# Gate and up products of an expert in one run, and its waiting steps in one place

## The chip, the cores and the metric

The kernel runs on one core of one Trainium2 chip. The time is device microseconds, the median of several runs. TensorE (PE) multiplies, VectorE (DVE) and ScalarE (ACT) work element by element, GpSimd (POOL) does small jobs, and SyncE (SP) issues the transfers (DMAs) from HBM. PSUM holds the products: eight banks of 128 partitions by 512 fp32.

## The reference

Two residual layers on 272 tokens of 1024 features: each has a token mixer, and then a channel mixer, which is a dense SwiGLU in layer 0 and eight experts in layer 1, of which each token uses two. The change is in the experts alone. For every expert e:

```python
def swiglu(x, wg, wu, wd):
    return (jax.nn.silu(x @ wg) * (x @ wu)) @ wd

for e in range(N_EXPERTS):                       # 8
    out = out + comb[:, e:e + 1] * swiglu(xt, wg[e], wu[e], wd[e])
```

`wg` and `wu` are 1024 x 3584, `wd` is 3584 x 1024, all fp32; `comb` holds the routing weights and is zero where a token doesn't use the expert. After the experts comes a last norm, of 256 tokens.

## The kernel before

**The stream of weights.** All weights come in the order of their use as units of 1 MiB (128 x 2048 fp32), one DMA each on SyncE's queue (class `Stream`). In the experts' stage sixteen buffers are used in turn (`raw`, `xh`, `xl`, `lt`, `mg`), and two units more land once in `nh` and `nl`. A buffer is free when `st.release(u)` is called behind the last matmul that reads it; the call also issues the next DMA into it, and SyncE waits there until TensorE has got so far. An expert has 42 units, 336 in all.

**An expert.** Each expert takes only the tokens that are routed to it, gathered into slots. Experts are ordered by their number of tokens. Those of kind "B" (0, 2, 3, 5, 6) have 96 slots, those of kind "S" (1, 4, 7) have 64. An expert goes through its hidden features in seven steps j of 512. The products of a step are gate (1024 features by 512, 2 units), up (the same) and down (512 by 1024, 2 units), in the order gate_up(0), gate_up(1), down(0), gate_up(2), down(1), ..., gate_up(6), down(5), down(6).

**Two ways through a product.** Weights are the moving operand, slots the stationary one. A unit has 4 blocks of 128 x 512, a product 8. Slots 1 to 64 are worked off by `halves`: per block two matmuls with 64 stationary columns, side by side in TensorE's columns. Slots 65 to 96 go through `quarters`: four with 32 columns. Each fp32 matmul leaves two records in the trace, so a product has 32 records of halves (L1214) and 64 of quarters (L1219). For a large expert `products` goes through the 8 blocks in one way and then in the other, and the next product begins in the way in which the last one ended (`turns`). For a small one there are halves only. A buffer is released in the second way over its blocks.

**Steps between.** `products` calls `between()` once, in a large expert between the two ways, in a small one after 4 blocks of 8. There stands other TensorE work: `hidden` transposes the last step's activations (L1316, 2 or 3 matmuls), which the next down product needs, and `spare_time(n)` takes n entries off the list `pending`. These are `by_slot` (L1109, and L1115 for expert 0: one-hot rows by slot, turned by TensorE), `scatter` (L1263: results of the expert before, added to the tokens), the ranking of the experts, and empty entries, which keep a scatter from being reached before its results are split:

```python
def between():
    if m and last:
        hidden(*last)
    spare_time(2 - m)
...
if not final and d == 0:
    pending.extend([lambda: None] * 2)
```

So a gate product has up to two entries in its middle, an up product the transposes and one, a down product one. Between the last two down products at the end of a group of experts stand the matmuls that gather the next group's tokens (L1089). The order on every engine is the program's; nothing is reordered.

Of the kernel before, what the change touches and what calls it, by code (L numbers as in the profile page):

```python
# [18 lines left out]
KD = D // P  # L19
# [15 lines left out]
SMALL = 64  # L35
MORE = CAP - SMALL
# [171 lines left out]
def _build(ctx, tc, nc, A, out, dbg):  # L208
    V, S, G, PE = nc.vector, nc.scalar, nc.gpsimd, nc.tensor
    w = A["w"]  # L210
    NRAW, NHL, NRAWB, NRAWC = 6, 3, 4, 2

    def units_of(pool, n):
        return [lambda: pool.tile([P, UNIT], F32, name="raw")] * n
# [26 lines left out]
    def bank(tag):  # L241
        return psum.tile([P, 512], F32, name=tag, bufs=BANKS[tag])
# [8 lines left out]
    st = Stream(nc, w, units_of(rawp, NRAW), hlp, NHL, 0, dbg.get("units", UNITS))  # L251
# [739 lines left out]
    def one(shape, dt, nm):  # L991
        return mo.tile(shape, dt, name=nm, bufs=1)

    acc = [[one([P, 512], F32, f"hacc{t}{d}") for d in range(2)] for t in range(2)]
# [46 lines left out]
    def spare_half(name):  # L1041

        return hlp.tile([P, HALF], F32R, name=name, bufs=NHL + (name == "whi"))

    pending = []
# [165 lines left out]
    def halves(a, x, w, start, stop):  # L1211

        for g in range(2):
            PE.matmul(a[g * SMALL:(g + 1) * SMALL, :256], lhsT=x, rhs=w[:, g * 256:(g + 1) * 256], start=start, stop=stop)  # L1214

    def quarters(a, x, w, start, stop):

        for r in range(4):
            PE.matmul(a[r * MORE:(r + 1) * MORE, 256:384], lhsT=x, rhs=w[:, r * P:(r + 1) * P], start=start, stop=stop,  # L1219
                      tile_position=(0, r * MORE))  # L1220

    turns = [0]

    def products(st, small, a, x, y, start, stop, between):

        blocks, u = st.pair()
        ways = [0] if small else [turns[0], 1 - turns[0]]
        for n, way in enumerate(ways):  # L1230
            for k, w in enumerate(blocks):
                if n == len(ways) - 1 and k == (4 if small else 0):
                    between()
                at, begin, end = a(k), start(k) and n == 0, stop(k) and n == len(ways) - 1
                if way:
                    quarters(at, y(k), w, begin, end)
                else:
                    halves(at, x(k), w, begin, end)
                if n == len(ways) - 1 and k % 4 == 3:
                    st.release(u + k // 4)  # L1240
        turns[0] = ways[-1]


# [2 lines left out]
    def split_y(run, q, d, a):  # L1246

        parts = []
        for y, n, c0, cw in ((YA, SMALL, 0, 256), (YB, MORE, 256, P))[:1 if run.small(q) else 2]:
            for i in range(P // n):  # L1250
                c = slice(i * cw, (i + 1) * cw)
                parts.append((y[:n, d, c], y[n:2 * n, d, c], a[i * n:(i + 1) * n, c0:c0 + cw]))
        for hi, lo, src in parts:
            S.activation(hi, src, AF.Copy)
        for hi, lo, src in parts:
            V.tensor_tensor(lo, src, hi.bitcast(F32), op=OP.subtract)
# [45 lines left out]
    pending = []  # L1302

    def experts(st, run, first):

        hid, dn_, oht = {}, {}, {}

        def hidden(q, j):

            h = hid.get((q, j), ())  # L1310
            if len(h) == 1:
                w = run.width(q)
                h.append(spare_half("whi")[:, :384].bitcast(F32))
                p = bank("acc")
                for b in range(w // P):
                    PE.transpose(p[:, b * P:(b + 1) * P], h[0][:, b * P:(b + 1) * P], ident)  # L1316
                V.tensor_copy(h[1][:, :w], p[:, :w])  # L1317

        def spare_time(n):
            for _ in range(n):  # L1320
                if pending:
                    pending.pop(0)()

        def gate_up(q, j, last):
            gu = []
            n, w = run.slots(q), run.width(q)
            x = run.x[q]

            for m in range(2):
                a = bank(("acc", "s")[m])  # L1330

                def between():
                    if m and last:
                        hidden(*last)
                    spare_time(2 - m)

                products(st, run.small(q), lambda k: a, lambda k: x[:, k, :SMALL], lambda k: x[:, k, SMALL:],
                         lambda k: k == 0, lambda k: k == KD - 1, between)
                gu.append(a)
            s = me.tile([P, 384], F32, name="es")  # L1340
            if first and q == 0:
                for i, c in enumerate((slice(0, 256), slice(256, 384))):
                    r = rs[:, i:i + 1]
                    S.activation(s[:, c], gu[0][:, c], AF.Silu, scale=r)
                    V.scalar_tensor_tensor(s[:, c], gu[1][:, c], r, s[:, c], op0=OP.mult, op1=OP.mult)
            else:
                S.activation(s[:, :w], gu[0][:, :w], AF.Silu)  # L1347
                V.tensor_tensor(s[:, :w], gu[1][:, :w], s[:, :w], op=OP.mult)  # L1348
            hid[q, j] = [s]

        def down(q, j, between):
            h = hid[q, j][1]

            def x(k):
                o = k % 2 * P + k % 4 // 2 * SMALL
                return h[:, o:o + SMALL]

            products(st, run.small(q), lambda k: dn_[q][k // 4], x, lambda k: h[:, 256 + k % 4 * MORE:256 + (k % 4 + 1) * MORE],
                     lambda k: j == 0 and k % 4 == 0, lambda k: j == FJ - 1 and k % 4 == 3, between)

        def results(q, d, final):

            split_y(run, q, d, dn_[q][d])
            if not final and d == 0:
                pending.extend([lambda: None] * 2)
            pending.extend([lambda t=t: scatter(run, q, oht[q], t, d, "acc" if final or t else "o") for t in range(2)])
            if final:
                pending.append(lambda: square_sums(d))

        for q in range(NEXP):  # L1370
            final = q == NEXP - 1
            i = run.group[q]
            turnover = q == run.groups[i][-1] and not final
            last = None
            oht[q] = mo.tile([P, 4 * P], F32R, name="oht")
            if q == 0:
                pending.append(lambda: run.by_slot(0, oht[0], first))
                if first:
                    ranking = rank_steps()
                    pending.extend([lambda: next(ranking)] * 8)  # L1380
            for j in range(FJ):
                gate_up(q, j, last)
                last = (q, j)
                if first and q == 0 and j == FJ - 4:
                    load_order()
                    for n in range(4):
                        pending.append(lambda n=n: again_by_tokens(n // 2, n % 2))
                if turnover and j == FJ - 2:
                    run.onehot(i + 1)
                if j == 0:  # L1390
                    continue
                if j == 1:
                    dn_[q] = [bank("t"), bank("t")]
                    if q:
                        pending.append(lambda q=q: run.by_slot(q, oht[q]))

                def between():
                    if j == FJ - 1:
                        hidden(q, j)
                    spare_time(1)  # L1400

                down(q, j - 1, between)
                if final and j == FJ - 2:
                    pending.extend([lambda d=d: g_final(d) for d in range(2)])
            if turnover:
                for c2 in range(4):
                    run.gather(i + 1, c2, ("s", "acc")[c2 % 2])
            if final:
                spare_time(len(pending))
                S.activation(mx_, ssq, AF.Sqrt)  # L1410
                XG["fin"] = st.spare().rearrange("p (t d f) -> p t d f", t=2, d=2)

            def between():
                if final and run.small(q):
                    results(q, 0, final)

            down(q, FJ - 1, between)
            for d in range(1 if final and run.small(q) else 0, 2):
                results(q, d, final)
        while pending:  # L1420
            pending.pop(0)()
        result()
# [147 lines left out]
```

## Time and profile before

| | |
|---|---|
| time, median of 3 runs | 1620.93 us (1620.39 to 1622.29) |
| the profiled execution | 1621.91 us, span 1620.2 us |
| TensorE busy | 1592.5 us (98%) |
| VectorE, ScalarE, GpSimd busy | 614.3, 464.5, 132.4 us |
| read from HBM | 468.93 MB |
| expert 0 begins | 752.70 us after the span's start |

Times in the rows below count from the span's start. A row of the timeline gives start, duration, engine, line, operation, what is written and read, the shape, and how many records are merged. Matmuls' ends are modelled, so starts are compared, not ends. The granted clock is a share of 2.4 GHz. The DMA share is the mean busy share of 16 DMA engines.

### The profile page before, as it was taken

The numbers are of one execution on the slowest core, as the hardware profiler recorded it, in microseconds if no ns is written. First come the engines' busy times: TensorE is split into PE (matmuls) and PEld (weight loads), VectorE is DVE, ScalarE is ACT, GpSimd is POOL, SyncE is SP. The second block draws the span as 40 slices with busy tenths as digits, with TensorE's granted clock in tenths as the row PEclk, the third lists the DMA queues.
The fourth block names the chain that finished last, engine by engine and source line by source line (L and its number), as shares of the span: only waits on it lengthen the run. The fifth ranks groups of instructions, "written<-read, shape, count | busy, mean of one in ns | idle before, by whom it ended". The sixth has DMA issues, their size and how long they took to land.

```text
span 1620.2 us, 41035 instructions
## 1 busy us (share of the span) xinstructions
PE 1592.5 (98%) x18251; PEld 1321.8 (82%) x18251; DVE 614.3 (38%) x1124; ACT 464.5 (29%) x811; POOL 132.4 (8%) x203
## 2 busy tenths in 40 slices
PE   8999999999999999999999999999999999999995
PEld 8999999999999999998777667777766677777663
DVE  5667676655556676764112111021020210210202
ACT  5545655544444446653011000010010100100101
POOL 3201152000012002430000000000000000000000
PEclk9999999999999999999999999999999999999998
DMA  7333454444453334766989999999999999999993
GB/s 304 120 141 131 151 186 161 179 176 166 179 189 138 131 130 158 272 256 240 371 329 359 419 418 417 417 418 417 405 400 419 418 418 417 418 417 407 405 419 153
DMA packets 66288, 472.78 MB, mean 292 GB/s; under 512 B 7344, under 2 KB 7472, under 8 KB 9520
## 3 DMA queue, kind: packets, MB, share of 16 engines
q1 hardware_dynamic: 65952, 469.86, 73.6%
q8 instruction: 147, 2.41, 0.6%
q14 instruction: 45, 0.37, 0.1%
q10 hardware_dynamic: 144, 0.15, 0.0%
HBM read 468.93 MB, written 1.05 MB: 290 GB/s over the span
## 4 chain that ended last, share of the span: by engine, by line
PE 95%; DVE 2%; ACT 1%; DMA 1%; POOL 0%; issue 0%; SPq 0%; ACTq 0%; DVEq 0%; POOLq 0%
PE s L1214 12%; PE t L1214 12%; PE acc L1214 12%; PE acc L280 8%; PE acc L282 8%; PE acc L281 8%; PE acc L1219 4%; PE s L1219 4%; PE t L1219 4%; PE s L282 2%; PE s L280 2%; PE s L281 2%; PE t L281 2%; PE t L280 2%; PE t L282 2%; PE acc L1316 2%
## 5 line engine op out<-in xcount | busy, mean ns | idle before, releaser
L167 DVE TENSOR_TENSOR wlo<-raw,whi 128x1024 fp32r<-128x1024 f32 x218 | 272.4, 1250 | 35.9 <-PE acc L282 13.5
L154 ACT ACTIVATE whi<-raw 128x1024 fp32r<-128x1024 f32 x218 | 229.4, 1055 | 155.7 <-issue 51.4
L280 PE MATMUL acc<-xh,whi 128*128 128x272 f32 (+1 forms) x864 | 252.9, 293 | 0.0
L282 PE MATMUL acc<-xh,wlo 128*128 128x272 f32 (+1 forms) x864 | 248.1, 287 | 0.8 <-DVE wlo L167 0.8
L281 PE MATMUL acc<-xl,whi 128*128 128x272 f32 (+1 forms) x864 | 247.6, 287 | 0.0
L1317 DVE COPY whi<-acc 128x384 f32<-128x384 f32 (+1 forms) x56 | 28.5, 508 | 500.5 <-PE acc L1316 500.5
L1347 ACT ACTIVATE es<-acc 128x384 f32<-128x384 f32 (+1 forms) x49 | 21.8, 444 | 554.8 <-PE acc L1316 538.4
L280 PEld LDWEIGHTS acc<-xh,whi 128*128 128x128 f32 x864 | 162.9, 189 | 1.6 <-issue 0.3
L282 PEld LDWEIGHTS acc<-xh,wlo 128*128 128x128 f32 x864 | 162.9, 189 | 1.0 <-DVE wlo L167 1.0
L281 PEld LDWEIGHTS acc<-xl,whi 128*128 128x128 f32 x864 | 163.2, 189 | 0.1
L1214 PE MATMUL s<-raw,xg 128*64 128x256 f32 x1344 | 156.8, 382 | 0.0
L1214 PE MATMUL t<-raw,whi 128*64 128x256 f32 x1328 | 153.1, 381 | 0.0
L1214 PE MATMUL acc<-raw,xg 128*64 128x256 f32 x1328 | 152.5, 380 | 0.0
L1214 PEld LDWEIGHTS s<-raw,xg 128*64 128x64 f32 x1344 | 93.8, 137 | 50.2 <-issue 6.1
L1214 PEld LDWEIGHTS acc<-raw,xg 128*64 128x64 f32 x1328 | 94.1, 137 | 49.2 <-issue 3.2
L1214 PEld LDWEIGHTS t<-raw,whi 128*64 128x64 f32 x1328 | 93.6, 137 | 48.5 <-issue 3.5
L280 PE MATMUL t<-xh,whi 128*128 128x272 f32 (+1 forms) x208 | 60.0, 288 | 0.0
L282 PE MATMUL t<-xh,wlo 128*128 128x272 f32 (+1 forms) x208 | 59.8, 288 | 0.0
L281 PE MATMUL t<-xl,whi 128*128 128x272 f32 (+1 forms) x208 | 59.8, 287 | 0.0
L1348 DVE TENSOR_TENSOR es<-s,es 128x384 f32<-128x384 f32 (+1 forms) x49 | 24.5, 501 | 92.3 <-PE s L1214 71.2
L1219 PE MATMUL acc<-raw,xg 128*32 128x128 f32 x1760 | 56.1, 279 | 0.0
L280 PE MATMUL s<-xh,whi 128*128 128x272 f32 (+1 forms) x176 | 52.0, 295 | 2.5 <-ACT whi L154 2.5
(453 smaller groups left out, 2650.7 us busy)
## 6 DMA issues: line engine op xcount, KB each, us to landing
raw<-w SPq DMA_DIRECT2D x356, 1024.0 KB, 12.4
xh<-w SPq DMA_DIRECT2D x21, 1024.0 KB, 17.5
xl<-w SPq DMA_DIRECT2D x21, 1024.0 KB, 17.0
lt<-w SPq DMA_DIRECT2D x21, 1024.0 KB, 17.8
mg<-w SPq DMA_DIRECT2D x21, 1024.0 KB, 18.3
raw<-w SPq DMA_DIRECT2D x6, 512.0 KB, 7.9
hT<-hT SPq DMA_DIRECT2D x4, 272.0 KB, 6.9
lw<-lruw SPq DMA_DIRECT2D x2, 512.0 KB, 8.9
```

What stands on the lines that cost most here:

```text
L154: self.nc.scalar.activation(hi, src, AF.Copy)
L167: self.nc.vector.tensor_tensor(lo, src, hi.bitcast(F32), op=OP.subtract)
L280: PE.matmul(ps, lhsT=wh, rhs=xh, start=start, stop=False)
L281: PE.matmul(ps, lhsT=wh, rhs=xl, start=False, stop=False)
L282: PE.matmul(ps, lhsT=wl, rhs=xh, start=False, stop=stop)
L1214: PE.matmul(a[g * SMALL:(g + 1) * SMALL, :256], lhsT=x, rhs=w[:, g * 256:(g + 1) * 256], start=start, stop=stop)
L1219: PE.matmul(a[r * MORE:(r + 1) * MORE, 256:384], lhsT=x, rhs=w[:, r * P:(r + 1) * P], start=start, stop=stop, tile_position=(0, r * MORE))
L1316: PE.transpose(p[:, b * P:(b + 1) * P], h[0][:, b * P:(b + 1) * P], ident)
L1317: V.tensor_copy(h[1][:, :w], p[:, :w])
L1347: S.activation(s[:, :w], gu[0][:, :w], AF.Silu)
L1348: V.tensor_tensor(s[:, :w], gu[1][:, :w], s[:, :w], op=OP.mult)
```

## The change

`products` takes a number n of pairs of units. The gate and up products of a step become one call with n = 2: sixteen blocks in one way, then sixteen in the other (for a small expert sixteen blocks of halves). Both PSUM banks are taken at the start. `between()` is called once for both, ahead of the second way or after 8 blocks of 16, and does the transposes and up to two entries. Buffers are released as before, in the last way over their blocks. A down product stays as it was. One empty entry less is put ahead of the scatters.

```diff
-    def products(st, small, a, x, y, start, stop, between):
+    def products(st, small, n, a, x, y, start, stop, between):
-        blocks, u = st.pair()
+        pairs = [st.pair() for _ in range(n)]
+        blocks = [w for b, _ in pairs for w in b]
         ways = [0] if small else [turns[0], 1 - turns[0]]
-        for n, way in enumerate(ways):
+        for i, way in enumerate(ways):
             for k, w in enumerate(blocks):
-                if n == len(ways) - 1 and k == (4 if small else 0):
+                if i == len(ways) - 1 and k == (4 * n if small else 0):
                     between()
-                at, begin, end = a(k), start(k) and n == 0, stop(k) and n == len(ways) - 1
+                at, begin, end = a(k), start(k) and i == 0, stop(k) and i == len(ways) - 1
                 if way:
                     quarters(at, y(k), w, begin, end)
                 else:
                     halves(at, x(k), w, begin, end)
-                if n == len(ways) - 1 and k % 4 == 3:
-                    st.release(u + k // 4)
+                if i == len(ways) - 1 and k % 4 == 3:
+                    st.release(pairs[k // 8][1] + k % 8 // 4)
         turns[0] = ways[-1]
...
         def gate_up(q, j, last):
-            gu = []
             n, w = run.slots(q), run.width(q)
             x = run.x[q]
-
-            for m in range(2):
-                a = bank(("acc", "s")[m])
-
-                def between():
-                    if m and last:
-                        hidden(*last)
-                    spare_time(2 - m)
-
-                products(st, run.small(q), lambda k: a, lambda k: x[:, k, :SMALL], lambda k: x[:, k, SMALL:],
-                         lambda k: k == 0, lambda k: k == KD - 1, between)
-                gu.append(a)
+            gu = [bank("acc"), bank("s")]
+
+            def between():
+                if last:
+                    hidden(*last)
+                spare_time(2)
+
+            products(st, run.small(q), 2, lambda k: gu[k // KD], lambda k: x[:, k % KD, :SMALL], lambda k: x[:, k % KD, SMALL:],
+                     lambda k: k % KD == 0, lambda k: k % KD == KD - 1, between)
...
-            products(st, run.small(q), lambda k: dn_[q][k // 4], x, lambda k: h[:, 256 + k % 4 * MORE:256 + (k % 4 + 1) * MORE],
+            products(st, run.small(q), 1, lambda k: dn_[q][k // 4], x, lambda k: h[:, 256 + k % 4 * MORE:256 + (k % 4 + 1) * MORE],
...
             if not final and d == 0:
-                pending.extend([lambda: None] * 2)
+                pending.append(lambda: None)
```

## Rows read from the trace of the kernel before

**Rows 1.** The page: span and number of instructions.
```profile
span 1620.2 us, 41035 instructions
```

**Rows 2.** Experts 0, 2: busy PE, PEld, DVE, ACT, POOL; clock, DMA share, GB/s.
```profile
752.00:879.00 127.00, 124.51 (x2076) 93.19 (x2079) 23.13 (x72) 12.27 (x29) 0.00 (x0) 0.97 0.87 334
...
958.00:1080.00 122.00, 122.00 (x2083) 90.51 (x2083) 15.06 (x32) 6.88 (x17) 0.00 (x0) 1.00 1.01 418
```

**Rows 3.** Issues of weights from 878.7 to 1575.2 us: time to landing.
```profile
DMA to landing us min/median/max: 5.2/19.8/21.2
```

**Rows 4.** Waits of SyncE's queue, 765 to 1600 us: total, times, longest.
```profile
SPq L126 <- DMA raw<-w: 227.0, 119, 2.9
```

**Rows 5.** The one issue at 878.8 us.
```profile
L126 SPq DMA_DIRECT2D raw<-w x1: 333/333/333, 878.8 to 878.8; - x1
...
DMA to landing us min/median/max: 5.2/5.2/5.2
```

**Rows 6.** The last issue of the stream.
```profile
L126 SPq DMA_DIRECT2D raw<-w x1: 333/333/333, 1574.8 to 1574.8; - x1
...
DMA to landing us min/median/max: 20.9/20.9/20.9
```

**Rows 7.** Timeline of TensorE in the last expert.
```profile
1546.21 3.62 PE L1214 MATMUL t<-raw,whi 128*64 128x256 f32 x32
1549.66 3.62 PE L1214 MATMUL acc<-raw,xg 128*64 128x256 f32 x32
...
1554.94 0.44 PE L1316 MATMUL acc<-ident,es 128*128 128x128 f32 x2
1555.31 1.95 PE L1214 MATMUL s<-xh,xg 128*64 128x256 f32 x16
...
1565.82 0.44 PE L1316 MATMUL acc<-ident,es 128*128 128x128 f32 x2
...
1594.06 5.40 PE L1214 MATMUL t<-raw,whi 128*64 128x256 f32 x48
```

**Rows 8.** Timeline of TensorE in expert 2: a run of quarters.
```profile
974.11 1.08 PE L1219 MATMUL acc<-raw,xg 128*32 128x128 f32 x32
...
975.01 1.06 PE L1219 MATMUL acc<-xh,xg 128*32 128x128 f32 x32
...
976.76 1.06 PE L1219 MATMUL s<-lt,xg 128*32 128x128 f32 x32
...
977.75 0.55 PE L1316 MATMUL acc<-ident,es 128*128 128x128 f32 x3
```

**Rows 9.** Timeline of TensorE: transposes with a scatter behind them.
```profile
1532.19 0.44 PE L1316 MATMUL acc<-ident,es 128*128 128x128 f32 x2
1532.39 0.71 PE L1263 MATMUL acc<-wlo,oht 128*128 128x512 f32 x2
1533.03 1.95 PE L1214 MATMUL s<-raw,xg 128*64 128x256 f32 x16
```

**Rows 10.** Timeline of TensorE in expert 0's first product; in brackets idle time before.
```profile
752.70 3.67 PE L1214 MATMUL acc<-raw,xg 128*64 128x256 f32 x32
758.18 0.99 PE L1109 MATMUL o<-ident,whi 128*128 128x128 f32 x4 [1.81 <-DVE whi L1105]
759.86 1.87 PE L1115 MATMUL o<-ssq,whi 128*128 128x1 f32 x8 [0.69 <-ACT oht L1110]
761.65 3.64 PE L1219 MATMUL acc<-raw,xg 128*32 128x128 f32 x64
...
767.13 1.08 PE L1214 MATMUL s<-raw,xg 128*64 128x256 f32 x8
```

**Rows 11.** A stretch of 2 us in it: the clock is the third number from the end.
```profile
760.00:762.00 2.00, 2.00 (x16) 1.97 (x20) 0.16 (x1) 0.00 (x0) 0.00 (x0) 0.50 1.04 442
```

**Rows 12.** The one issue at 1197.1 us, at the end of expert 3.
```profile
L126 SPq DMA_DIRECT2D raw<-w x1: 333/333/333, 1197.1 to 1197.1; - x1
...
DMA to landing us min/median/max: 8.4/8.4/8.4
```

## The prediction, made before the change was run

> **What bounds the kernel now.** I read the table of stretches first, then the DMA issues one at a time, and then TensorE's timeline. All of the change lies in the experts' stage, which runs from 752.7 us almost to the end of the span [rows 1]. The reader is to see two things there. TensorE has no free time: in expert 2 it is busy for the whole stretch, 122.00 of 122.00 us [rows 2]. And the DMA engines have none either from expert 1 on: their share in that same stretch is 1.01 at 418 GB/s [rows 2], which is 2.51 us for one 1 MiB unit of weights. In the first expert alone they have room (0.87, 334 GB/s).
>
> So the question is which of the two sets the end. The issues answer it. Of the units issued between 878.8 and 1574.8 us the median takes 19.8 us to land [rows 3], nearly eight units' worth of queue, and SyncE waits 227 us for earlier transfers [rows 4]. One unit with an empty queue ahead of it takes 5.2 us: the one issued at 878.8, at the end of expert 0 [rows 5]. From that issue on the queue is never empty, so DMA time runs from there to the last landing, 1574.8 + 20.9 = 1595.7 us [rows 6], whatever TensorE does. Before it, issues wait for TensorE to free a buffer. At the far end TensorE's last run of halves, 48 records over three units, starts at 1594.06 [rows 7]; its third unit is read from about 1594.06 + 2 x 1.75 = 1597.6. That is 1.9 us after it landed.
>
> Hence two paths lead to the end. TensorE's: the sum of its work. The DMA's: the moment at which expert 0 has freed its last buffers, plus a fixed time for the units still to come, plus the tail. They are 1.9 us apart now, with TensorE the later. A TensorE gain after expert 0 is worth at most 1.9 us; a gain within expert 0 moves both.
>
> **The change, part by part.**
>
> *Fewer runs of one tiling.* A run of halves costs 3.45 us per 32 records (1546.21 to 1549.66) [rows 7]. The run from 1555.31 to the transposes at 1565.82 holds 96 records and takes 10.51 where 3 x 3.45 = 10.36 would do: 0.15 for entering and leaving. Quarters cost 1.75 us per 64 in mid-run (975.01 to 976.76) [rows 8], and the run of 128 from 974.11 to 977.75 takes 3.64 where 3.50 would do: 0.14. By the code an expert with 96 slots changes its way 21 times now and 14 times afterwards. Counting the runs in the order in which they are issued, with the steps between them, I get 88 of halves and 53 of quarters before, 64 and 37 after. That is 40 runs less, of which 36 in the five large experts: 24 x 0.15 + 16 x 0.14 = 5.8 us. In expert 0 alone it is 5 and 3, 1.2 us.
>
> The Trainium skill says that changing the tiling mode drains TensorE (TensorEngine Tiling (Array Packing), Tiling Modes, Key Properties), and puts a drain at about 128 cycles (TensorE: Matmul & The Clock Gate, Phases on the wall clock), which I estimate at 0.05 us at full clock. By that figure the 40 runs would be worth 2.1 us, and the result would come about 1 us less low; the rows show three times as much per run, and I go by them.
>
> *Steps that stand together.* Transposes followed by halves take 0.37 us (1554.94 to 1555.31) [rows 7], and followed by a scatter 0.20 (1532.19 to 1532.39) [rows 9]. Each group of steps merged with another saves 0.17. The same counting gives 82 groups before and 74 after: 1.4 us, none of it in expert 0.
>
> *The first by_slot step.* It stands in the middle of expert 0's first gate product now. Halves begin at 752.70 and would be through at 756.2, then TensorE stands still for 1.81 us, until VectorE has written the one-hot rows (758.18) [rows 10]. The granted clock then falls to its lower level, 1.2 GHz (0.50 at 760 to 762) [rows 11]. The step takes 3.47 us (758.18 to 761.65) [rows 10], and the 128 quarters after it 5.48 (761.65 to 767.13) where 3.63 is the rule: 1.85 lost. Afterwards sixteen blocks of halves come first (7.06 us, to 759.8), so VectorE is done 1.4 us before the step is reached. The wait goes (1.81), the quarters run at full clock (1.85), and the step itself shrinks. Its 0.69 us wait for ScalarE [rows 10] stays, and its records halve at most: from 3.47 to between 2.1 and 3.5. I take 2.4, so 1.1 gained. Together 4.8 us, all in expert 0.
>
> *What is added.* No instruction is. The second PSUM bank is taken 3.45 to 7 us earlier; its former reader is a product pair back, so this costs nothing. One empty entry less stands ahead of the scatters, so in a small expert the first comes behind 8 blocks of halves and not 12 (3.6 us after the previous expert's last product, not 5.3). I charge nothing, since the split that it waits for takes the same time from that product's first four blocks; without that cover the wait is 1.7 us at most, three times. Gate units are freed later in the large experts: with quarters first, the first one after 3.5 + 0.5 + 1.73 = 5.7 us of its group, not 3.5. That is 2.2 us later on SyncE's queue, behind which the next issues stand. Queued transfers cover it: where the queue is shortest, at 1197 us, a unit still takes 8.4 us to land [rows 12], against 5.2 unqueued.
>
> **The sum.** TensorE's path: 5.8 + 1.4 + 4.8 = 12.0 us less. Expert 0 has 1.2 + 4.8 = 6.0 of it. Its last product now ends with halves and not quarters, which frees its first unit 0.8 us sooner (a unit of halves takes 1.73, one of quarters 0.87), so the DMA's path begins 6.8 us sooner (the DMA engines have 0.13 x 127 = 16 us of room in that stretch to move the same units [rows 2]). With the DMA's path at -6.8 and TensorE's at -12.0, the DMA's is the later one at the end. TensorE has to wait for the last unit, and 1.8 of the 1.9 us between landing and use go as well: 6.8 + 1.8 = 8.6 us. The profiled execution took 1621.91 us, so 1613.3; it stood 1.0 us over the median of the runs (1620.93), and against that I predict **1612.3 us**. The other 3.4 us of TensorE's gain turn into waits for weights, at the beginnings of experts 2 and 5, and in the last expert.
>
> **The rivals.**
>
> *The clock stays low or falls elsewhere.* The step's 0.69 us wait stays in expert 0 and may bring the same drop a little later; for it speaks that a still stretch of 1.81 us went before the drop [rows 10, 11], against it that the stretch is now a third as long, behind 7 us of matmuls. The two losses at low clock, 1.85 and 1.1, come back: 1612.3 + 2.95 = about 1615.3. The Trainium skill has a kernel whose clock falls at each DMA wait between bursts of matmuls (TensorE: Matmul & The Clock Gate, HAM oscillation); the waits that I expect at the end would be of that kind, and no run here shows one yet. In the last expert units arrive every 2.5 us and take 1.73 to use, so TensorE would stand still for 0.8 of every 2.5 us, and a fall there would be partly covered by that waiting. Chance 0.17.
>
> *The DMA's path doesn't start sooner,* because something else than TensorE paces the issues in expert 0. For it speaks only that the share is already 0.87. Then the 1.9 us alone are to be had: 1619.1. Chance 0.12.
>
> *TensorE's whole gain counts,* if transfers run a little faster than in this profile: 1608.9. Chance 0.08.
>
> *The ring runs dry: slower.* Later freeing eats the queue in the second of two large experts in a row. It decides where a landing time falls under 5.2 + 2.2 = 7.4 us; 8.4 is the shortest seen. If the engines stood idle 2.2 us in each of the 14 groups of experts 3 and 6, that is 31 us, less the 8.6: about 1643. Against it: TensorE gains on the DMA up to there, which frees buffers sooner. Chance 0.08.
>
> **How the numbers follow.** The forecast has 0.55. The unknowns in it (the step 1.4 either way, waits up to 3 x 1.7 where they aren't covered, the run-to-run spread of 1.9) make its own range 1610 to 1615. Reaching down to the third rival and up over the first gives 1608.5 to 1617.5, leaving out 0.20. A change of 0.2%, 3.2 us, is about what a measurement of this kernel can tell from none: faster 0.80, same 0.12 (the second rival), slower 0.08 (the fourth).
>
> **What would show it.** The first by_slot step right behind 64 halves, without an idle stretch, and no low clock near 760 us. Experts' runs of up to 96 halves and 192 quarters. The last issue of expert 0 near 872 us with the queue still short, the last landing near 1589, and TensorE waits for weights in the last expert where there were none. It is wrong if the last landing stays near 1595, if landings take under 7 us in experts 3 or 6, or if the clock row shows a low stretch inside the stage.

## The result, and the profile after

The changed kernel is slower: 1639.06 us in the median of 4 runs (1637.80 to 1642.62) against 1621.28 for the kernel before on the same chip, a ratio of 1.0115 with a 95% interval of 1.0103 to 1.0127. I had predicted 1612.3, in a range that ended at 1617.5. The profiled execution took 1639.19 us, 17.3 more than the one of before.

The page's span, and its row for the queue that fetches instructions:

```profile
span 1637.4 us, 41015 instructions
...
q8 instruction: 147, 2.41, 0.6%
```

TensorE executes as many matmuls as before (18251 in both profiles). The stretches of experts 0 and 2, answering [rows 2], and of the 2 us where the clock had been low, answering [rows 11] (busy PE, PEld, DVE, ACT, POOL; then clock, DMA share, GB/s):

```profile
753.00:876.00 123.00, 120.33 (x2081) 91.13 (x2081) 22.87 (x72) 12.59 (x30) 0.00 (x0) 1.00 0.87 344
957.00:1079.00 122.00, 117.15 (x2027) 87.99 (x2027) 14.22 (x30) 6.23 (x14) 0.00 (x0) 1.00 1.01 418
...
760.00:762.00 2.00, 1.31 (x12) 0.69 (x9) 0.00 (x0) 0.60 (x1) 0.00 (x0) 1.00 0.81 332
```

The low clock near 760 us is gone (1.00 where it was 0.50). But in expert 2 TensorE, which had been busy for all of 122.00 us, now stands idle for 4.85 of them. What it waits for from 752 us to the end (who waits <- for whom: total us, times, longest):

```profile
PE s L1219 <- issue: 11.6, 11, 1.7
PE o L1109 <- DVE whi L1105: 5.8, 7, 0.9
PE acc L1317 <- issue: 2.1, 2, 1.4
PE acc L1264 <- DVE wlo L1257: 1.2, 2, 1.0
PE acc L1214 <- issue: 0.7, 2, 0.5
PE o L1115 <- ACT oht L1110: 0.7, 1, 0.7
...
```

Three of these rows, 14.4 us in 15 places, end in "issue": the instruction came late without any wait that the profile shows. The kernel before has none of them there. Its one large wait, 1.81 us for VectorE [rows 10], is gone; in its place are 5.8 us in 7 waits for the same line of VectorE.

TensorE in expert 0's first product pair, answering [rows 10]:

```profile
753.36 3.67 PE L1214 MATMUL acc<-raw,xg 128*64 128x256 f32 x32
756.86 3.62 PE L1214 MATMUL s<-raw,xg 128*64 128x256 f32 x32
760.42 0.66 PE L1109 MATMUL o<-ident,whi 128*128 128x128 f32 x4
761.76 1.05 PE L1115 MATMUL o<-ssq,whi 128*128 128x1 f32 x8 [0.69 <-ACT oht L1110]
762.74 1.95 PE L1219 MATMUL acc<-raw,xg 128*32 128x128 f32 x64
```

The step stands behind 64 halves and takes 2.32 us (760.42 to 762.74; 3.47 before), without a wait ahead of it. In expert 2 a run of 256 quarters (964.03 to 973.06) shows one of the new waits, among its last 32 records; the run of 128 in [rows 8] passes without one:

```profile
968.42 1.06 PE L1219 MATMUL acc<-xh,xg 128*32 128x128 f32 x32
969.29 1.06 PE L1219 MATMUL s<-xl,xg 128*32 128x128 f32 x32
970.16 0.60 PE L1219 MATMUL s<-lt,xg 128*32 128x128 f32 x10
972.27 0.86 PE L1219 MATMUL s<-lt,xg 128*32 128x128 f32 x22 [1.51 <-issue]
```

And the merged steps a little later, where by_slot follows transposes:

```profile
988.46 1.93 PE L1219 MATMUL s<-raw,xg 128*32 128x128 f32 x64
990.32 0.55 PE L1317 MATMUL acc<-ident,es 128*128 128x128 f32 x3
991.78 0.81 PE L1109 MATMUL o<-ident,whi 128*128 128x128 f32 x4 [0.91 <-DVE whi L1105]
992.52 3.67 PE L1214 MATMUL acc<-raw,xg 128*64 128x256 f32 x32
```

The issue at the end of expert 0 and the last issue of all, answering [rows 5, 6]:

```profile
L126 SPq DMA_DIRECT2D raw<-w x1: 333/333/333, 875.1 to 875.1; - x1
...
DMA to landing us min/median/max: 4.9/4.9/4.9
...
L126 SPq DMA_DIRECT2D raw<-w x1: 333/333/333, 1589.6 to 1589.6; - x1
...
DMA to landing us min/median/max: 19.8/19.8/19.8
```

The last unit lands at 1609.4 us. TensorE's last run of halves starts at 1611.20, so its third unit is read from about 1614.7 (two units of halves at 1.75 us later): 5.3 us of slack, where there were 1.9.

**Where the time went.** I took the starts of TensorE's records from the first expert matmul (752.70 before, 753.36 after) to the first scatter behind the last run of halves (1599.66, 1616.80), run by run, and compared each run's length with its usual one (3.45 us per 32 halves, 1.75 per 64 quarters, 0.15 or 0.14 for entering). The stage grew from 846.96 to 863.44 us:

| term | predicted, us | found, us |
|---|---|---|
| 24 runs of halves and 16 of quarters fewer | -5.8 | -5.9 |
| first by_slot: wait, clock, step | -4.8 | -4.8 |
| steps that stand together | -1.4 | +7.1 |
| runs longer than usual, nearly all at an "issue" wait | 0 | +20.1 |
| sum on TensorE's path | -12.0 | +16.5 (stage: +16.5) |

The 20.1 us are more than the view's 14.4, since it counts only what lies behind the modelled end of the matmul ahead. All 15 waits lie in quarter runs or directly behind them: in all 5 runs of 256 records, in or behind 10 of 25 runs of 192, and in none of 128.

### The profile page after: what moved, and what is told of

Read it like the earlier page. It is cut to its first block, busy times and chain, and to the rows that moved or that the text cites. A ratio compares the mean times of both kernels' runs of the same rounds, so it can differ in the third digit from the quotient of the medians.

```text
span 1637.4 us, 41015 instructions
## 1 busy us (share of the span) xinstructions
PE 1591.2 (97%) x18251; PEld 1324.1 (81%) x18251; DVE 613.4 (37%) x1124; ACT 464.1 (28%) x811; POOL 132.2 (8%) x203
## 3 DMA queue, kind: packets, MB, share of 16 engines
q8 instruction: 147, 2.41, 0.6%
## 4 chain that ended last, share of the span: by engine, by line
PE 94%; POOL 1%; issue 1%; DVE 1%; ACT 1%; DMA 1%; SPq 0%; ACTq 0%; DVEq 0%; POOLq 0%
PE acc L1214 12%; PE s L1214 12%; PE t L1214 12%; PE acc L280 8%; PE acc L282 8%; PE acc L281 8%; PE t L1219 4%; PE s L1219 4%; PE acc L1219 4%; PE s L280 2%; PE s L282 2%; PE s L281 2%; PE t L280 2%; PE t L281 2%; PE t L282 2%; PE acc L1317 2%
## 5 line engine op out<-in xcount | busy, mean ns | idle before, releaser
L1219 PE MATMUL s<-raw,xg 128*32 128x128 f32 x1760 | 57.1, 273 | 8.4 <-issue 8.4
L1219 PEld LDWEIGHTS s<-raw,xg 128*32 128x32 f32 x1760 | 49.9, 110 | 10.6 <-issue 10.6
## 6 DMA issues: line engine op xcount, KB each, us to landing
xh<-w SPq DMA_DIRECT2D x21, 1024.0 KB, 14.4
```

## The experiments

**What the two theories are.** Each of the waits has a packet of the instruction queue just ahead of or in it. The DMA queues' packets, MB and share, from 969.8 to 972.3 us around the wait above, and from 964 to 969.8 ahead of it:

```profile
q1 hardware_dynamic: 138, 1.01, 98.1%
q8 instruction: 1, 0.02, 2.7%
...
q1 hardware_dynamic: 343, 2.47, 102.7%
```

In the second stretch there is no packet of instructions. Theory A: TensorE's instructions come by DMA, some 16 KB at a time (147 packets, 2.41 MB), between the weights' packets; a long run of quarters uses them faster than they come. A run of 64 quarters is 128 instructions (each matmul has its weight load) in 1.75 us, so one in 13.7 ns, against one in 54 ns in halves (64 in 3.45 us). The rivals: sixteen blocks hold their buffers longer and starve the DMA queue; steps that stand together cost the time; long quarter runs are slow in themselves.

**e1_light: the changed kernel with little weight traffic.** Units of experts 1 to 7 are transferred with a quarter of their columns, and the matmuls read that quarter four times, so the output isn't the reference's.

```
+        elif self.next_dma >= DENSE_UNITS + EXP_UNITS:
+            self.nc.sync.dma_start(t[:, :512], self.src(self.next_dma)[:, :512])
...
+        if self.cur >= 2 * (DENSE_UNITS + EXP_UNITS):
+            o = 0
```

> The changed kernel, but each unit of weights of experts 1 to 7 is transferred with a quarter of its columns, and the matmuls read that quarter four times (so the output isn't the reference's; TensorE's instructions are the same in number, shape and order). Theory A (TensorE runs out of instructions in long runs of quarters, because their refill waits among the weights' transfers): TensorE's waits that the profile ends with "issue", 14.4 us in 15 places in the changed kernel, fall under 3 us, and the time to about 1622 us. Theory B (the refill has its own pace, whatever the other transfers do): about 14 us stay, 1639 us.

Measured: 1620.83 us in one run, where the kernel before took 1620.33 on that chip. The same expert 2 (clock, DMA share and GB/s last), and two rows of the waits:

```profile
957.00:1079.00 122.00, 121.09 (x2085) 91.12 (x2083) 15.24 (x34) 8.87 (x23) 0.00 (x0) 1.00 0.29 93
```

```profile
PE o L1114 <- DVE whi L1110: 5.8, 7, 0.9
...
PE acc L1322 <- issue: 1.0, 1, 1.0
```

The waits at issue fall from 14.4 us to 1.0 with the same instructions in the same runs. The waits for VectorE stay. So the former hang on the traffic; the latter don't.

**e2_short: sixteen blocks, but quarter runs of 128 at most.** The call for two products stays, and each call takes halves first.

```
-        ways = [0] if small else [turns[0], 1 - turns[0]]
+        ways = [0] if small else [0, 1]
```

> The changed kernel, but every product begins with halves. A step is then 16 blocks of halves, 16 of quarters, 8 of halves, 8 of quarters: no run of quarters over 128 records, while gate and up are still one call with their buffers held as long. Theory A and B (instructions run out in long runs of quarters): no issue waits of TensorE over 0.3 us; 20 us less for them, and 70 runs more at 0.145 us, so about 1629 us. Rival (sixteen blocks in one call do the harm, by holding buffers or banks): the waits stay, and 1649 us.

Measured: 1628.55 us (1627.64 to 1629.27), ratio 1.0047 (1.0030 to 1.0064). No wait at issue is left, 5.8 us for VectorE are. Buffers are still held for sixteen blocks, so this rival falls. What is left above the kernel before are the merged steps, and 99 runs of halves and 70 of quarters where it has 88 and 53.

**e3_steps: the kernel before with the steps' places alone changed.**

```
-                    spare_time(2 - m)
+                    spare_time(2 * m)
...
-                pending.extend([lambda: None] * 2)
+                pending.append(lambda: None)
```

> The kernel before, with only the places of the steps changed: none in a gate product, transposes and up to two entries in the up product, one empty entry less. My account of the change has three parts: issue waits in long runs of quarters (20 us more), by_slot behind the transposes, whose one-hot rows VectorE makes only after it has copied the transposes (7 waits of 1.0 us more), and less of runs, merged steps and expert 0's first wait (11 us less). By it this kernel has no issue waits, the seven waits of by_slot and the gain in expert 0 of 4.8 and of merged steps: about 1623 us. Rival (steps standing together cause the issue waits): some 14 us of them, 1637 us or more.

Measured: 1623.57 us (1622.78 to 1626.89), ratio 1.002 (1.001 to 1.003), no wait at issue. So steps that stand together don't make the instruction waits. But they make the VectorE waits (5.8 us again), and these eat the gain of the first by_slot step, which e3 has too. The profiled execution took 1625.65 us, 2.1 over the median. Expert 0 began in it at the lower clock, though TensorE shows no wait ahead of it, and its first 32 records of halves took 5.29 us and not 3.60 (the granted clock is third from the end):

```profile
753.00:757.00 4.00, 4.00 (x22) 2.42 (x23) 2.94 (x13) 2.04 (x4) 0.00 (x0) 0.57 0.07 25
```

**e4_swap: the changed kernel with the entries ahead of the transposes.** VectorE copies the transposes out of PSUM, and only then makes the one-hot rows for a by_slot that comes behind them; with by_slot first there is nothing to wait behind.

```
             def between():
+                spare_time(2)
                 if last:
                     hidden(*last)
-                spare_time(2)
```

> The changed kernel, but the entries go first in the middle and the transposes after them. By my account VectorE makes by_slot's one-hot rows before it has to wait for the transposes, so the seven waits (5.8 us at the matmul, 7.5 us with what the merged steps should have cost) go: 1631 to 1633 us, with the issue waits as they were. Rival (the waits are for something else, such as a free buffer of the one-hot rows or a PSUM bank): no change, 1639 us.

Measured: 1636.06 us (1635.33 to 1639.49), ratio 1.0101 (1.0084 to 1.0118): 3 us less than the changed kernel in the medians, 2.1 in the profile's stage (861.36 for 863.44), and the intervals of the two ratios overlap. The 6 to 8 us expected are not there. The waits show why; there is no row of by_slot's any more, but:

```profile
PE s L1219 <- issue: 13.8, 11, 2.2
PE acc L1317 <- issue: 3.7, 2, 2.0
```

The mechanism was right and the size off: VectorE's waits went (5.8 us), and the instruction waits grew from 14.4 to 17.9. The stretches behind two of these waits are also at the lower clock, for 3.4 us each; the first of them, with the granted clock third from the end:

```profile
1184.00:1190.00 6.00, 5.58 (x36) 3.38 (x38) 0.56 (x1) 0.00 (x0) 0.00 (x0) 0.72 0.60 229
```

**e7_wide: half the instructions for the same quarters.** Where e1 takes the traffic away, this takes instructions away and leaves the traffic: two matmuls of 256 columns for a block in place of four of 128.

```
-        for r in range(4):
-            PE.matmul(a[r * MORE:(r + 1) * MORE, 256:384], lhsT=x, rhs=w[:, r * P:(r + 1) * P], ...
+        for g in range(2):
+            r = 2 * odd + g
+            PE.matmul(a[r * MORE:(r + 1) * MORE, 256:512], lhsT=x, rhs=w[:, g * 256:(g + 1) * 256], ...
```

> The changed kernel, with a block's quarter product written as two matmuls of 256 columns in place of four of 128; even blocks use one pair of column groups of the array, odd blocks the other, so that four run side by side as before. The same columns, weights read, runs and steps, half the instructions in each quarter run. The two partial sums are not added up, so the output is not the reference's. Theory A (TensorE uses its instructions faster than they are fetched beside the weights' traffic): a run of 256 records is now one of 128, which showed no wait; the issue waits (14.4 us) go, the by_slot waits (5.8) stay: 1639 - 14.4 = about 1624, down to 1620 if quarters run no slower. Theory B (a long stretch of quarters is itself slowed, by its columns or by reading its weights while others are written): the waits in the quarter runs stay, about 1639.

Measured: 1616.56 us (1615.76 to 1617.48), ratio 0.9972 (0.9961 to 0.9983). The run that had the wait at 972.27 is this one, 32 records where there were 64:

```profile
961.33 1.93 PE L1220 MATMUL acc<-raw,xg 128*32 128x256 f32 x32
963.08 1.91 PE L1220 MATMUL s<-raw,xg 128*32 128x256 f32 x32
964.81 1.05 PE L1220 MATMUL acc<-raw,xg 128*32 128x256 f32 x16
...
967.40 1.05 PE L1220 MATMUL s<-lt,xg 128*32 128x256 f32 x16
968.38 0.55 PE L1319 MATMUL acc<-ident,es 128*128 128x128 f32 x3
```

```profile
PE o L1109 <- DVE whi L1105: 5.8, 7, 0.9
PE acc L1266 <- DVE wlo L1259: 1.2, 2, 1.0
...
q8 instruction: 121, 1.98, 0.5%
```

The run takes 7.05 us (961.33 to 968.38), as four times 1.75 should, and there is no wait at issue anywhere in the stage, at the same traffic. The stage is 841.03 us, 22.4 less than after the change: the 20.1 us and a little more. So it is neither the quarters' columns nor the reading of the experts' weights. The packets give the unit: 3360 matmuls and as many loads fewer are 26 packets fewer (147 to 121), 258 instructions each.

The places of the waits in the program settle it. Counted over TensorE's weight loads and matmuls from the first in the trace, all 15 instruction waits of the changed kernel stand at the same point of a block of 256 (the count is 193 or 194 past a multiple of 256), and each ends 1.3 to 1.6 us after a packet of the instruction queue has ended. The 15 of e4_swap stand at that point too. The blocks of 256 that end in such a wait last 4.2 to 5.6 us in the changed kernel and 3.4 to 4.8 in e1_light, 17.7 us less in all; all other blocks of the stage together differ by 0.5 us.

The starts of the packets show how fast they come. Between 880 and 1600 us the smallest distance between two of them is 6.03 us in the kernel before, and 39 of 80 distances there lie between 6.03 and 7; in e1_light, with little traffic, the distance goes down to 3.38. In the changed kernel 9 of 79 are under 6 us. The two shortest, 4.4 us from 1116.4 and from 1446.1, lie where the DMA share has fallen to 0.89 and 0.83; but one of 5.0 us, from 1184.1, has a share of 1.02, so 6 us is usual beside the full traffic and not a fixed floor. A long run of quarters uses 256 instructions in 3.5 us, sooner than such a packet comes. A run of 128 records is 256 instructions in all, and the halves behind it use theirs four times more slowly; that it lives on what is in stock is argued, for no run shows the stock itself. The Trainium skill (Runtime: NRT & Kernel Launch, Instruction fetch mechanics) says that engines refill in blocks of 256 instructions and 16 KiB, which the packets confirm, and that the refill is hidden because an engine dispatches more slowly than it fills; beside saturated weights' traffic the trace says otherwise, and it decides.

**e5_first: the first by_slot step alone.** The kernel before, with the step moved to the middle of the up product.

```
             if q == 0:
+                pending.extend([lambda: None] * 2)
                 pending.append(lambda: run.by_slot(0, oht[0], first))
```

> The kernel before, with two empty entries put ahead of expert 0's first by_slot step, so that it stands in the middle of the up product and not of the gate product; every run of matmuls keeps its length. The one part of the change from which the theory expects a gain that lasts: the 1.81 us wait for VectorE, the low clock behind it (1.85) and about 1.1 of the step go, on TensorE's path and, since it all lies in expert 0, on the DMA's too: 1620.3 - 4.8 = 1615.5 us, and no stretch of lower clock near 760 us. Rival: the DMA's path does not start sooner when TensorE is sooner in expert 0, then at most the 1.9 us of slack are to be had: 1618.5 or more.

Measured: 1617.87 us (1616.02 to 1619.60), ratio 0.9981 (0.9972 to 0.9990), against 1621.35 for the kernel before: 3.5 us in the medians, and 4.86 in the profile's stage (842.10 for 846.96). The step follows quarters without a wait:

```profile
758.65 1.93 PE L1219 MATMUL s<-raw,xg 128*32 128x128 f32 x64
760.51 0.66 PE L1109 MATMUL o<-ident,whi 128*128 128x128 f32 x4
761.86 1.05 PE L1115 MATMUL o<-ssq,whi 128*128 128x1 f32 x8 [0.69 <-ACT oht L1110]
762.84 3.67 PE L1214 MATMUL s<-raw,xg 128*64 128x256 f32 x32
```

The interval on the ratio (1.6 to 4.5 us) reaches neither clearly past the rival's 1.9 nor to the expected 4.8, so the times alone don't part them. The profile does: the last unit, issued at 1572.1, lands at 1592.1, 3.6 us before that of [rows 6]. The DMA's path did begin sooner with TensorE's.

**e6_order: e3's steps, with the entries ahead of the transposes.** Runs stay as short as before the change.

```
+                    spare_time(2 * m)
                     if m and last:
                         hidden(*last)
-                    spare_time(2 * m)
```

> e3_steps with the entries ahead of the transposes: runs of matmuls as in the kernel before (no quarter run over 128), steps in the up product alone, by_slot no longer directly behind the transposes. Theory: e3's by_slot waits (5.8 us in 7 groups) go and no wait for instructions comes in their place as it did in e4, for there is no long run of quarters: 1623.6 - 5.8 = 1617.8, to 1615.5 if the first step's gain is then seen whole. Rival: it is the steps' standing together that cost the time, in whatever order: about 1623.

Measured: 1616.39 us (1615.24 to 1616.75), ratio 0.9970 (0.9959 to 0.9981). It is the fastest of these kernels, 5.0 us under the kernel before. by_slot now stands ahead of the transposes and waits for nothing:

```profile
988.03 3.62 PE L1214 MATMUL s<-raw,xg 128*64 128x256 f32 x32
991.59 0.66 PE L1109 MATMUL o<-ident,whi 128*128 128x128 f32 x4
992.08 0.49 PE L1316 MATMUL acc<-ident,es 128*128 128x128 f32 x3
992.50 1.95 PE L1219 MATMUL s<-raw,xg 128*32 128x128 f32 x64
```

So steps may stand together; it is their order that made the 5.8 us of waits. Beside the first by_slot step, the groups of steps take 0.9 us less in all than in the kernel before, where I had expected 1.4. In e6's chain of waits the last of the long pieces is a transfer (start, us), and TensorE waits for weights at the end:

```profile
1505.62 3.63 PE t L1219 x128
1571.49 20.63 DMA raw<-w
```

```profile
PE t L1214 <- DMA raw<-w: 0.2, 1, 0.2
```

The last unit lands just as it is used, where there were 1.9 us between the two.

## Why the prediction was wrong

*What bounds the kernel* held where the queue of transfers stayed filled. From the issue of [rows 5], the end of expert 0, to the last landing it is 716.9 us in the kernel before, 717.6 in e5_first and 717.8 in e6_order. In e6_order TensorE gained more than 1.9 us without the new waits: the slack at the last unit went to nothing, and a transfer entered the chain. e7_wide, which has the change without the instruction waits, issues that unit at 872.4 us, where I had said near 872, and its last landing is at 1586.8, where I had said near 1589.

*Fewer runs of one tiling* held, count and price: -5.9 us for -5.8. I was wrong on the lengths, though: I wrote of runs of up to 192 quarters, and at the beginning of each large expert, where two pairs follow each other without a down product, there are 256.

*What is added* is the step that failed: "No instruction is." That is so, and I costed the longer runs at nothing but the tiling's change. Yet a run of 64 quarters draws 128 instructions in 1.75 us, and runs that had been at most 128 records became 192 and 256. Their instructions then came too late: 20.1 us, shown by the traffic (e1_light), by the number of instructions (e7_wide), by the length of the run (e2_short) and by the places of the waits, 256 instructions or a multiple of it apart. No wait of this kind stood in the trace of before, so no row priced it; but the page has a queue of its own for instructions, and I didn't ask how often it has to deliver.

*Steps that stand together* failed too: +7.1 where I had -1.4. I priced the change of tiling saved and did not ask what by_slot would wait for in its new place: VectorE's copy of the transposes ahead of it and then the one-hot rows. I had named VectorE's lateness in expert 0 and didn't carry the question to the other seven. e6_order shows that order, not the merging, set this: there it is -0.9.

*The first by_slot step* held: its wait and the low clock went, and 4.8 us with them (e5_first: 4.86 in the stage by itself); the step takes 2.32 us, where I had taken 2.4. Yet expert 0 as a whole became only 3.5 us shorter (123.28 us to expert 1's first matmul, 126.79 before) and not 6.0, for two instruction waits stand in it, and its last issue came at 875.1, not near 872.

*The rivals.* None of the four happened. The only one on the slower side had transfers starve. Its sign came: landing times fell to 4.7 us, as short as with an empty queue [rows 5], and from the end of expert 0 to the last landing it took 734.3 us. (The shortest of the trace before, past the end of expert 0, is also not the 8.4 us that I named but 7.9, at 1192.7.) But TensorE never waited for weights in the changed kernel. e7_wide frees its buffers in the same order without the instruction waits: its landings come down to 6.5 us only, and it doesn't wait for weights either. e3_steps, which frees them as before the change, comes down to 6.3. So the short queue is mostly TensorE's own lateness, and it costs nothing here. A lower clock inside the stage appears in e4_swap, where it follows instruction waits, and in the profile of e3_steps, at the start of expert 0; in the changed kernel it doesn't.

What stays open: why the packets seldom come closer than some 6 us where the weights' share is 1.01. Each takes about 1.07 us there and 0.97 in e1_light, so it isn't the packet's own transfer; the queueing ahead of it is likely, and wasn't measured by itself. Nor does a run show why e3_steps began expert 0 at the lower clock.

## What to carry to other kernels

Making runs of small matmuls longer saves what the change of tiling costs (0.15 us here), but asks more of the instruction supply: compare the instructions that the run uses per microsecond with how often the instruction queue delivered in a stretch of the same DMA load. Put matmuls that use instructions slowly between bursts of quick ones, or write the burst with fewer and wider matmuls. And before steps are put together, look at which engine feeds each of them: a step whose input another engine makes belongs ahead of one that gives that same engine work.

## What the runs showed of the hardware

- TensorE took in 256 instructions per packet (258 by the difference of two kernels), and all 30 of its instruction waits in two kernels stand at the same point of a block of 256. The packets started no oftener than every 6.03 us in the kernel before, at a DMA share of 1.01, and as often as every 3.38 us in e1_light, where the share in expert 2 was 0.29.
- A TensorE that uses 256 instructions in 3.5 us beside some 418 GB/s of weights stopped for up to 1.7 us in the changed kernel and 2.2 in e4_swap; the trace calls that "issue".
- In e4_swap such stops were followed twice by 3.4 us at the lower clock (0.72 granted over 6 us); in the changed kernel, with stops of up to 1.7 us, they never were.
